# Retention's sample tokens in a hybrid decode step: keys copied to their placed columns ahead of the products, v summed and placed by one matrix

## The chip, the cores and the metric

One Trainium2 chip, one core. The metric is the device time of one execution in microseconds (us), the median of several runs. The core's engines run side by side, each through its own list of instructions in order: TensorE (PE for its matmuls, PEld for the loads of the stationary matrix), VectorE (DVE), ScalarE (ACT), GpSimd (POOL) and SyncE (SP), which here only issues transfers. Engines wait for each other through semaphores.

## The reference, cut to what matters

A two-layer decoder step with shared weights: a prompt of 512 tokens, and 32 sample tokens (8 sequences of 4 tokens each, at positions from 4096). Layer 1 mixes by retention, with 4 heads, keys of 256 and values of 512 elements; each sample sequence has a state `S` of 256 x 512 per head.

```python
def step(S, qkv):
    qc, kc, vc = qkv
    scores = jnp.einsum('bhid,bhjd->bhij', qc, kc) * decay
    inner = jnp.einsum('bhij,bhjv->bhiv', scores, vc)
    cross = jnp.einsum('bhid,bhdv->bhiv', qc, S) * cross_w[:, :, None]
    S_new = S * chunk_decay[:, None, None] + jnp.einsum('bhjd,bhjv->bhdv', kc * state_w[:, :, None], vc)
    return S_new, inner + cross
```

`q`, `k` (after a rotation by position) and `v` are projections of the normalized tokens. For a sample sequence there is one chunk of its 4 tokens. The outputs are all tokens after the decoder, the convolution states and the retention states, among them `S_new` of the eight sample sequences.

## The kernel before, in words

The kernel keeps tokens along the free side: 512 prompt columns and 32 sample columns, 544 in all. Each projection is made in three products of a high and a low part: a tensor is split into a rounded high part (`split`: ScalarE copies to the reduced type, L202) and the rest (VectorE subtracts, L203), and high x high, high x low and low x high are summed in PSUM. A scheduler orders the instructions of each engine from the program; `tc.issue_after` adds an order by hand.

The retention layer runs over the four heads, `h` from 0 to 3. In a head:

- `value` (its products stand on L1251 to L1253) multiplies the tokens by four pieces of the v weights, 24 products of 512 columns each, into four banks of PSUM. After each second piece it multiplies the sample tokens `xs` by the unsplit pieces (L1259), four products side by side in four strips of 32 output rows, so that the sum over the depth lies in four partial sums, one to a strip, in `pvs`. After the second piece it splits q and k, and calls `sample_scores` and `keys`. At the end `pvs` is scaled and split into `v4` (L1283, L1284), the four strips are added by the product with `sum4` (L1288), and the sum, 32 rows, is split into `v2`. Then the prompt's v is split into `vh`, `vl` (L1294, L1295).
- `sample_scores` multiplies the 32 sample keys by the 32 sample queries (L1434), masks and scales the result (`ss`, L1438 and L1439), splits it, and places it by two products with `places` (L1151, L1152, in `placed`) into 128 rows; ScalarE copies it to `scp` (L1443).
- `keys` transposes the prompt's keys (L1306) and splits them into `knh`, `knl`, and transposes the sample keys (L1315) and splits them into `k2`.
- `sample_operands` places `v2` and `k2` by four products with `places` (L1151, L1152), copies the first to `vs` (L1350) and multiplies the second by two row masks into `kns` (L1353).
- `state` makes the prompt's state (L175 to L177), `scores` its masked scores, `inner` its outputs.
- `sample_outputs` multiplies `vs` by `scp` (L1459) and the states by the queries `qm` (L1463); `states_update` adds `kns` times `vs` (L1481) to the scaled states (L1486, VectorE) and stores them.
- In heads 1 and 2 (`AHEAD`) the head before is projected in between (`held_parts`, which splits the gated outputs into `oldh`, `oldl`; `held_project`, L187), and each head but the last makes the next head's q (`qk_project`, L187).

The 128 placed rows are four groups of 32, for two sequences each, in places of 8 rows: for group g the rows hold the 8 tokens of the group three times over, and 8 rows of zeros. With v's places (high, low, high) and k's places (high, high, low) one product over a group's rows sums high x high, high x low and low x high. `places` holds four such placing matrices of 32 x 128 (two for v, two for k), loaded as a part of the constants `cb` into `where_p`.

```python
here = (n[:, None] // 8 == j[None] // 32) & (n[:, None] % 8 == j[None] % 8)
place = (j[None] % 32) // 8
for w, at in enumerate(((0, 2), (1,), (0, 1), (2,))):
    cb[:NS, 800 + w * P : 800 + (w + 1) * P] = here & np.isin(place, at)
```

PSUM has four single banks (`bank`, named sm) and two double ones (`psum`, named mm). `pvs` holds one double tile through all of `value`; the scores' tile, the prompt's transposed keys and the sample's transposed keys follow each other in the other. `where_p` and `mask_p` lie in a stretch of `cb` that the jobs ahead of this layer use as a weight buffer, so their loads (L1175, in `qk_loaded`) wait until that buffer is free.

Of the kernel before, what the change touches and what calls it, by code (L numbers as in the profile page):

```python
# [52 lines left out]
def hybrid_decode_kernel(ctx: ExitStack, tc: tile.TileContext, a: dict, o: dict):  # L53
# [1062 lines left out]
    with ExitStack() as c2:  # L1116
# [18 lines left out]
        part4 = one.tile([P, 2, NS], F32, tag="part4", name="part4")  # L1135
        for i in range(2):
            nc.vector.tensor_add(
                part4[:, i, :], ident[:, 2 * i * NS : (2 * i + 1) * NS], ident[:, (2 * i + 1) * NS : (2 * i + 2) * NS]
            )
        nc.vector.tensor_add(sum4, part4[:, 0, :], part4[:, 1, :])  # L1140
# [7 lines left out]

        def placed(out, hi, lo, w):

            nc.tensor.matmul(out, places[:, 2 * w, :], hi, start=True, stop=False)  # L1151
            nc.tensor.matmul(out, places[:, 2 * w + 1, :], lo, start=False, stop=True)  # L1152
# [15 lines left out]
        def qk_loaded(st):  # L1168
# [5 lines left out]
            for t, c in columns[:3]:  # L1174
                nc.sync.dma_start(t, a["cb"][:, c])  # L1175

            with tc.issue_after(last_mixed[0].ins):
# [6 lines left out]
                nc.vector.tensor_copy(places, where_p[:NS].rearrange("p (w c) -> p w c", w=4))  # L1184
# [54 lines left out]
        def value(h, st):  # L1239
# [47 lines left out]
            for i in range(2):  # L1287
                nc.tensor.matmul(pvs[:NS, 1, :], sum4, v4[:, i, :], start=(i == 0), stop=(i == 1))  # L1288
            v2 = [pool.tile([NS, DV], F32R, tag=f"rt{i}", name=nm("v2"), bufs=1) for i, pool in enumerate((kp, tp))]
            v2_split[0] = split(*v2, pvs[:NS, 1, :])  # L1290
# [8 lines left out]
            st["v"] = (vh, vl, v2)  # L1299

        def keys(h, st):
# [12 lines left out]
            for dt in range(2):  # L1314
                nc.tensor.transpose(pt[:NS, 0, token_tiles(dt)], krot[:, dt, SEQ:], ident)  # L1315
            k2 = qp.tile([NS, 2, 2 * P], F32R, tag="vs", name=nm("k2"), bufs=1)
            split(k2[:, 0, :], k2[:, 1, :], pt[:NS, 0, : 2 * P])
            st["kn"] = (knh, knl, k2)

        def state(h, st, c):  # L1320

            knh, knl, k2 = st["kn"]
            vh, vl, v2 = st["v"]
# [19 lines left out]

        def sample_operands(h, st):
            k2, v2 = st["kn"][2], st["v"][2]
            pt = psum()
            placed(pt[:, 0, :], *v2, 0)
            placed(pt[:, 1, : 2 * P], k2[:, 0, :], k2[:, 1, :], 1)
            vs = qp.tile([P, DV], F32R, tag="vs", name=nm("vs"), bufs=1)
            nc.scalar.activation(vs, pt[:, 0, :], AF.Copy)  # L1350
            kns = tp.tile([P, 2, 2 * P], F32R, tag="kns", name=nm("kns"), bufs=1)
            for r in range(2):
                nc.vector.tensor_scalar_mul(kns[:, r, :], pt[:, 1, : 2 * P], mask_r[:, r : r + 1])  # L1353
            st["vs"], st["kns"] = vs, kns
# [36 lines left out]
        def inner(h, st, it):  # L1391

            vh, vl, _ = st["v"]
# [35 lines left out]
        def sample_scores(h, st):  # L1429
# [3 lines left out]
            for dt in range(2):  # L1433
                nc.tensor.matmul(  # L1434
                    pt[:NS, 0, :NS], krot[:, dt, SEQ:], qrot[:, dt, SEQ:], start=(dt == 0), stop=(dt == 1)
                )
            ss = tp.tile([NS, NS], F32, tag="ss", name=nm("ss"), bufs=1)
            nc.vector.tensor_mul(ss, pt[:NS, 0, :NS], mask_s[:NS])  # L1438
            nc.vector.tensor_mul(ss, ss, st["gs"][:NS])  # L1439
# [105 lines left out]
        for h in range(NH):  # L1545
# [205 lines left out]
```

## Time and profile before

| | |
|---|---|
| runs | 1411.15, 1411.09 and 1410.4 us; median 1411.09 |
| profiled execution, first to last instruction | 1409.1 us |
| median of the runs less that span | 2.0 us |
| TensorE busy, matmuls | 1396.3 us, 99% |
| VectorE busy | 1132.7 us, 80% |
| ScalarE busy | 821.7 us, 58% |
| GpSimd busy | 213.9 us, 15% |
| granted TensorE clock, mean | 0.999 |

The profile is of one execution, which carries no time of its own beside its span. A row of the timeline has the start in us from the span's start, the time of the row in us, the engine, the line of the kernel, the operation, the tile written and the tiles read, for a matmul the shape of the array that it uses (rows*columns), the partitions x elements written, the type, and the number of instructions put together in the row. In brackets stands how long the engine was idle before it and what ended that. A float32 product whose operands aren't of the reduced type stands as two matmuls for each one of the program (L1259, L1434, L1463); a transpose is one. The retention heads lie from about 690 to 1010 us.

### The profile page before, as it was taken

Reading aid. Unit: us, or ns where it says so; the run is one execution under the profiler, and the core shown is the slowest. Engines: PE = TensorE matmul, PEld = TensorE weight load, DVE = VectorE, ACT = ScalarE, POOL = GpSimd, SP = SyncE. Lnnn points to the kernel's source line nnn. Section 1 sums busy time; section 2 is a strip of 40 time slices with the busy share of each in tenths; the row PEclk is TensorE's granted clock in tenths of the full one; section 3 lists DMA queues with packets and bytes.
Section 4 is the critical chain, followed back from the end, with each engine's and each line's share of the span. In section 5 each row is a group of like instructions: output and inputs, shape, how many; then the busy total and the mean of one; then the engine's idle time right before and its main releaser. Section 6 shows DMA issues by size and latency. Waiting matters only on the chain.

```text
span 1409.1 us, 26606 instructions
## 1 busy us (share of the span) xinstructions
PE 1396.3 (99%) x10476; PEld 1319.9 (94%) x10476; DVE 1132.7 (80%) x1929; ACT 821.7 (58%) x1281; POOL 213.9 (15%) x248
## 2 busy tenths in 40 slices
PE   9999999999999999999999999999999999999997
PEld 9999999999999999999877877887899999999997
DVE  6987879898989878767867586585798898989884
ACT  7666567677677557677532313213387767667654
POOL 0111011222221204111000000000111222121212
PEclk9999999999999999999999999999999999999999
DMA  6476347768686745677666365465676777777742
GB/s 206 121 166 166 107 110 158 173 163 185 143 196 149 171 108 158 176 199 203 197 216 232 120 212 179 139 240 179 201 152 151 168 170 172 154 184 157 163 108 87
DMA packets 99246, 233.82 MB, mean 166 GB/s; under 512 B 9744, under 2 KB 33312, under 8 KB 98736
## 3 DMA queue, kind: packets, MB, share of 16 engines
q1 hardware_dynamic: 67984, 167.60, 38.3%
q0 software_dynamic: 28688, 56.61, 23.5%
q10 hardware_dynamic: 2448, 7.91, 1.5%
q8 instruction: 82, 1.34, 0.4%
q14 instruction: 44, 0.36, 0.1%
HBM read 191.97 MB, written 28.42 MB: 156 GB/s over the span
## 4 chain that ended last, share of the span: by engine, by line
PE 93%; DVE 4%; DMA 1%; ACT 1%; issue 1%; POOL 0%; SPq 0%; DVEq 0%; POOLq 0%; ACTq 0%
PE sm L386 43%; PE mm L386 16%; PE mm L187 14%; PE sm L187 4%; PE sm L1251 2%; PE sm L1252 2%; PE sm L1253 2%; PE sm L175 2%; PE sm L177 2%; PE sm L176 1%; PE sm L1463 1%; DVE S L1486 1%; PE mm L1259 1%; PE mm L1412 0%; DVE ol L203 0%
## 5 line engine op out<-in xcount | busy, mean ns | idle before, releaser
L386 PE MATMUL sm<-oh,wh 128*128 128x272 f32 x856 | 247.8, 290 | 0.5 <-DVE b L447 0.5
L386 PE MATMUL sm<-ol,wh 128*128 128x272 f32 x856 | 246.2, 288 | 0.0
L386 PE MATMUL sm<-oh,wl 128*128 128x272 f32 x856 | 246.1, 287 | 0.0
L202 ACT ACTIVATE h<-w 128x1024 fp32r<-128x1024 f32 (+3 forms) x170 | 136.6, 804 | 105.8 <-PE mm L386 92.7
L203 DVE TENSOR_TENSOR l<-w,h 128x1024 fp32r<-128x1024 f32 (+3 forms) x170 | 153.5, 904 | 28.0 <-ACT h L202 25.0
L315 ACT ACTIVATE wh<-w 128x1024 fp32r<-128x1024 f32 (+1 forms) x134 | 133.7, 998 | 56.0 <-PE sm L386 48.3
L386 PEld LDWEIGHTS sm<-oh,wh 128*128 128x128 f32 x856 | 161.3, 188 | 2.0 <-DVE b L447 0.9
L386 PEld LDWEIGHTS sm<-oh,wl 128*128 128x128 f32 x856 | 161.1, 188 | 0.0
L386 PEld LDWEIGHTS sm<-ol,wh 128*128 128x128 f32 x856 | 160.9, 188 | 0.1
L386 PE MATMUL sm<-parts,wh 128*128 128x272 f32 x736 | 142.5, 288 | 0.0
L202 ACT ACTIVATE wh<-w 128x1024 fp32r<-128x1024 f32 (+3 forms) x76 | 67.6, 897 | 117.2 <-PE mm L187 62.0
L318 POOL DMA_DIRECT2D wl<-in_ffgu_dram x87 | 81.9, 941 | 327.9 <-ACT wl L317 135.5
L386 PE MATMUL mm<-oh,h 128*128 128x272 f32 x396 | 115.5, 292 | 0.0
L386 PEld LDWEIGHTS sm<-parts,wh 128*128 128x128 f32 x736 | 115.5, 188 | 0.0
L386 PE MATMUL mm<-oh,l 128*128 128x272 f32 x396 | 113.4, 286 | 0.0
L386 PE MATMUL mm<-ol,h 128*128 128x272 f32 x396 | 113.2, 286 | 0.0
L316 DVE TENSOR_TENSOR wl<-w,wh 128x512 fp32r<-128x512 f32 (+1 forms) x134 | 87.1, 650 | 26.5 <-ACT wh L315 26.2
L386 PE MATMUL sm<-parts,wl 128*128 128x272 f32 x368 | 106.1, 288 | 0.2 <-DMA wl<-in_rtqk_dram 0.2
L317 ACT ACTIVATE wl<-wh 128x512 fp32r<-128x512 f32 (+1 forms) x173 | 102.9, 595 | 2.0
L203 DVE TENSOR_TENSOR wl<-w,wh 128x1024 fp32r<-128x1024 f32 (+3 forms) x76 | 79.5, 1055 | 13.4 <-ACT wh L202 13.0
L187 PE MATMUL mm<-parts,wh 128*128 128x272 f32 x488 | 82.6, 291 | 0.9 <-ACT wh L202 0.9
L386 PE MATMUL sm<-oh,h 128*128 128x272 f32 x284 | 82.3, 290 | 0.3 <-ACT oh L202 0.2
(382 smaller groups left out, 3841.2 us busy)
## 6 DMA issues: line engine op xcount, KB each, us to landing
w<-in_ffgu_dram SPq DMA_DIRECT2D x66, 512.0 KB
wl<-in_ffgu_dram POOLq DMA_DIRECT2D x87, 256.0 KB, 5.2
S<-in_rets_dram SPq DMA_DIRECT2D x16, 1024.0 KB
out_rets_dram<-S SPq DMA_DIRECT2D x16, 1024.0 KB
w<-in_ffdn_dram SPq DMA_DIRECT2D x36, 384.0 KB
cb<-in_ffgu_dram SPq DMA_DIRECT2D x22, 512.0 KB
w<-in_cvin_dram SPq DMA_DIRECT2D x21, 512.0 KB
wl<-in_ffdn_dram POOLq DMA_DIRECT2D x48, 192.0 KB, 4.7
```

The lines of the kernel that those rows point to most:

```text
L175: nc.tensor.matmul(out, lh, rh, start=start, stop=False, skip_group_check=True)
L177: last_product[0] = nc.tensor.matmul(out, ll, rh, start=False, stop=stop, skip_group_check=True)
L187: last_product[0] = nc.tensor.matmul(half(pt, hf)[:, :HT], w[:, c], act[k][:, hf * HT : (hf + 1) * HT], start=(first and k == ks[0] and i ...
L202: h = nc.scalar.activation(dh, src, AF.Copy)
L203: last_low[0] = nc.vector.tensor_sub(dl, src, dh.bitcast(F32))
L315: nc.scalar.activation(wh, w, AF.Copy)
L316: last_mixed[0] = nc.vector.tensor_sub(wl[:, :n], w[:, :n], wh[:, :n].bitcast(F32))
L317: nc.scalar.activation(wl[:, n:], wh[:, n:].bitcast(F32), AF.Copy, scale=-1.0)
L318: nc.gpsimd.dma_start(wl[:, n:], src[:, 1, :] if len(src.shape) == 3 else src[:, n:], accum_op=ALU.add)
L386: last = nc.tensor.matmul(out, w[:, c], b, start=(first and j == 0 and i == 0), stop=(j == len(self.ks) - 1 and i == 2), skip_group_check= ...
L1251: nc.tensor.matmul(out, xh[kt][:, ts_], wh[:, cw], start=(kt == 0), stop=False)
L1252: nc.tensor.matmul(out, xh[kt][:, ts_], wl[:, cw], start=False, stop=False)
```

## The change

The score of the sample tokens is now made in 128 rows at once: ScalarE copies the rotated sample keys three times over to their placed columns in `kpl` (128 x 2 x 4 x 4 x 8, zeros in each fourth place), and the products with the queries (new L1452) give the placed scores. The transposes of the sample keys (new L1330) read `kpl` too and give placed keys. `v4` is multiplied by one 128x128 matrix `put` in place of `sum4`: it adds the four strips and puts the sum in all three places. High and low parts are then made from the placed results by row scales: ScalarE rounds the result times `sign` (1, -1 or 0 by row; for low rows the negative high part), and VectorE adds the result times a row mask for the low rows. `mask_put`, the score mask in placed rows, is made once, in head 0, by a product with `put`. `sample_operands`, `placed`, `places`, `k2` and `v2` go. `where_p` is loaded in four pieces of 32 partitions, the two v placing matrices for each strip, in place of all four for 32 rows; `put` is their sum.

```diff
-        places = one.tile([NS, 4, P], F32R, tag="places", name="places")
-
-        sum4 = one.tile([P, NS], F32R, tag="sum4", name="sum4")
...
-        nc.vector.tensor_add(sum4, part4[:, 0, :], part4[:, 1, :])
+        put = one.tile([P, P], F32R, tag="put", name="put")
+        kpl = one.tile([P, 2, 4, 4, 8], F32, tag="kpl", name="kpl")
+        nc.gpsimd.memset(kpl, 0.0)
+        mask_put = one.tile([P, NS], F32, tag="mput", name="mput")
+        place = one.tile([P, 4], F32, tag="place", name="place")
+        nc.vector.tensor_reduce(
+            place, ident.rearrange("p (g q c) -> p q g c", g=4, q=4), axis=mybir.AxisListType.XY, op=ALU.add
+        )
...
+        def signs():
+
+            both = one.tile([P, 1], F32, tag="both", name="both")
+            nc.gpsimd.tensor_tensor(both, place[:, 0:1], place[:, 2:3], op=ALU.add)
+            nc.gpsimd.tensor_tensor(sign[:, 0:1], both, place[:, 1:2], op=ALU.subtract)
+            nc.gpsimd.tensor_tensor(both, place[:, 0:1], place[:, 1:2], op=ALU.add)
+            nc.gpsimd.tensor_tensor(sign[:, 1:2], both, place[:, 2:3], op=ALU.subtract)
+            nc.gpsimd.tensor_tensor(sign[:, 2:4], mask_r, sign[:, 1:2].to_broadcast([P, 2]), op=ALU.mult)
+            nc.gpsimd.tensor_tensor(low_k, mask_r, place[:, 2:3].to_broadcast([P, 2]), op=ALU.mult)
...
-            for t, c in columns[:3]:
+            for t, c in (columns[0], columns[2]):
                 nc.sync.dma_start(t, a["cb"][:, c])
+            for g in range(4):
+                nc.sync.dma_start(where_p[g * NS : (g + 1) * NS, : 2 * P], a["cb"][:NS, 800 : 800 + 2 * P])
+            signs()
...
-                nc.vector.tensor_copy(places, where_p[:NS].rearrange("p (w c) -> p w c", w=4))
+                nc.vector.tensor_add(put, where_p[:, :P], where_p[:, P : 2 * P])
...
             for i in range(2):
-                nc.tensor.matmul(pvs[:NS, 1, :], sum4, v4[:, i, :], start=(i == 0), stop=(i == 1))
-            v2 = [pool.tile([NS, DV], F32R, tag=f"rt{i}", name=nm("v2"), bufs=1) for i, pool in enumerate((kp, tp))]
-            v2_split[0] = split(*v2, pvs[:NS, 1, :])
+                nc.tensor.matmul(pvs[:, 1, :], put, v4[:, i, :], start=(i == 0), stop=(i == 1))
+            vt = kp.tile([P, DV], F32R, tag="rt0", name=nm("vt"), bufs=1)
+            vs = st["vs"] = qp.tile([P, DV], F32R, tag="vs", name=nm("vs"), bufs=1)
+            v2_split[0] = nc.scalar.activation(vt, pvs[:, 1, :], AF.Copy, scale=sign[:, 0:1])
+            nc.vector.scalar_tensor_tensor(
+                vs, pvs[:, 1, :], place[:, 1:2], vt.bitcast(F32), op0=ALU.mult, op1=ALU.add
+            )
...
             for dt in range(2):
-                nc.tensor.transpose(pt[:NS, 0, token_tiles(dt)], krot[:, dt, SEQ:], ident)
-            k2 = qp.tile([NS, 2, 2 * P], F32R, tag="vs", name=nm("k2"), bufs=1)
-            split(k2[:, 0, :], k2[:, 1, :], pt[:NS, 0, : 2 * P])
+                nc.tensor.transpose(pt[:, 0, token_tiles(dt)], kpl[:, dt].rearrange("p g q c -> p (g q c)"), ident)
+            kns = st["kns"] = tp.tile([P, 2, 2 * P], F32R, tag="kns", name=nm("kns"), bufs=1)
+            kt = tp.tile([P, 2, 2 * P], F32R, tag="rt1", name=nm("kt"), bufs=1)
+            for r in range(2):
+                nc.scalar.activation(kt[:, r, :], pt[:, 0, : 2 * P], AF.Copy, scale=sign[:, 2 + r : 3 + r])
+            for r in range(2):
+                nc.vector.scalar_tensor_tensor(
+                    kns[:, r, :], pt[:, 0, : 2 * P], low_k[:, r : r + 1], kt[:, r, :].bitcast(F32),
+                    op0=ALU.mult, op1=ALU.add,
+                )
...
-        def sample_operands(h, st):
...
-            placed(pt[:, 0, :], *v2, 0)
-            placed(pt[:, 1, : 2 * P], k2[:, 0, :], k2[:, 1, :], 1)
...
             for dt in range(2):
+                nc.scalar.activation(
+                    kpl[:, dt, :, :3, :],
+                    krot[:, dt, SEQ:].rearrange("p (g c) -> p g c", g=4).unsqueeze(2).to_broadcast([P, 4, 3, 8]), AF.Copy,
+                )
+            if h == 0:
+                nc.tensor.matmul(pt[:, 1, :NS], put[:NS].bitcast(F32), mask_s[:NS], start=True, stop=True)
+                nc.scalar.activation(mask_put, pt[:, 1, :NS], AF.Copy)
+            for dt in range(2):
                 nc.tensor.matmul(
-                    pt[:NS, 0, :NS], krot[:, dt, SEQ:], qrot[:, dt, SEQ:], start=(dt == 0), stop=(dt == 1)
+                    pt[:, 0, :NS], kpl[:, dt].rearrange("p g q c -> p (g q c)"), qrot[:, dt, SEQ:],
+                    start=(dt == 0), stop=(dt == 1),
                 )
-            ss = tp.tile([NS, NS], F32, tag="ss", name=nm("ss"), bufs=1)
-            nc.vector.tensor_mul(ss, pt[:NS, 0, :NS], mask_s[:NS])
-            nc.vector.tensor_mul(ss, ss, st["gs"][:NS])
-            s2 = tp.tile([NS, 2, NS], F32R, tag="s2", name=nm("s2"), bufs=1)
-            split(s2[:, 0, :], s2[:, 1, :], ss)
-            placed(pt[:, 1, :NS], s2[:, 0, :], s2[:, 1, :], 1)
-            nc.scalar.activation(grouped(scp)[:, :, 0:8], grouped(pt[:, 1, :NS]), AF.Copy)
+            ss = tp.tile([P, NS], F32, tag="ss", name=nm("ss"), bufs=1)
+            nc.vector.tensor_mul(ss, pt[:, 0, :NS], mask_put)
+            nc.vector.tensor_mul(ss, ss, st["gs"])
+            s2 = tp.tile([P, NS], F32R, tag="s2", name=nm("s2"), bufs=1)
+            nc.scalar.activation(s2, ss, AF.Copy, scale=sign[:, 1:2])
+            nc.vector.scalar_tensor_tensor(
+                grouped(scp)[:, :, 0:8], grouped(ss), place[:, 2:3], grouped(s2.bitcast(F32)), op0=ALU.mult, op1=ALU.add
+            )
...
             fill(0)
-            sample_operands(h, st)
             state(h, st, 0)
```

In the order that the scheduler makes of the changed kernel, the score products take the place of the old ones in heads 1 to 3, right behind L1259; the eight transposes of the prompt's keys follow two value products behind them in every head. In head 0 the product of `mask_put` stands behind L1259 and two value products ahead of the scores. In heads 1 and 2 VectorE makes the second half of `oldl` ahead of the low half of the fourth v piece, where it stood behind it and behind one further weight split.

More of the change, by code (lines that the diff above doesn't have):

```diff
@@ L1314, in keys @@
             for dt in range(2):
[L1315 to L1318 removed]
+                nc.tensor.transpose(pt[:, 0, token_tiles(dt)], kpl[:, dt].rearrange("p g q c -> p (g q c)"), ident)
[8 more added lines that the diff above has]
+                )
+            st["kn"] = (knh, knl)
         def state(h, st, c):
[L1322 to L1323 removed]
+            knh, knl = st["kn"]
+            vh, vl = st["v"]
             if c == 0:
```

22 lines of the change are left out of this document (4 added, 18 removed).

## The prediction

> **What bounds the kernel now.** I read the page's busy times and chain first, then the busy times by stretch for the four heads of the retention layer (690 to 1010 us), where every edit lies.
>
> ```profile
> PE 1396.3 (99%) x10476; PEld 1319.9 (94%) x10476; DVE 1132.7 (80%) x1929; ACT 821.7 (58%) x1281; POOL 213.9 (15%) x248
> ...
> PE 93%; DVE 4%; DMA 1%; ACT 1%; issue 1%; POOL 0%; SPq 0%; DVEq 0%; POOLq 0%; ACTq 0%
> ```
>
> ```profile
> 729.00:766.00 37.00, 36.84 (x231) 28.38 (x228) 34.61 (x60) 5.77 (x6) 3.17 (x5) 1.00 0.70 232
> ...
> sum 320.00, PE 319.29 PEld 249.62 DVE 222.50 ACT 89.29 POOL 12.60; mean PE 45.61 PEld 35.66 DVE 31.79 ACT 12.76 POOL 1.80
> ```
>
> The columns of a stretch are its length, then PE, PEld, DVE, ACT and POOL busy, granted clock, DMA share and GB/s. TensorE is idle for 0.71 us of these 320 us, at full clock; VectorE has 97 us to spare and ScalarE 231. So TensorE's stream of instructions sets the end, and an edit is worth what it takes out of that stream, unless it makes a new wait. Busy matmul rows overlap each other, so I price by the distance from one start to the next, in the timeline of TensorE. Here is head 0 around the scores of the sample tokens:
>
> ```profile
> 701.97 1.06 PE L1259 MATMUL mm<-w,xs 128*32 128x512 f32 x8
> 702.86 0.29 PE L1434 MATMUL mm<-rot,rot 128*32 128x32 f32 x4
> 703.07 0.50 PE L1251 MATMUL sm<-wh,parts 128*128 128x512 f32 x1
> 703.41 0.40 PE L1252 MATMUL sm<-wl,parts 128*128 128x512 f32 x1
> ...
> 703.88 0.40 PE L1251 MATMUL sm<-wh,parts 128*128 128x512 f32 x1
> 704.20 0.28 PE L1151 MATMUL mm<-s,places 32*128 32x32 f32 x1
> 704.41 0.50 PE L1252 MATMUL sm<-wl,parts 128*128 128x512 f32 x1
> 704.84 0.28 PE L1152 MATMUL mm<-s,places 32*128 32x32 f32 x1
> 705.05 0.50 PE L1253 MATMUL sm<-wh,parts 128*128 128x512 f32 x1
> 705.39 0.40 PE L1251 MATMUL sm<-wh,parts 128*128 128x512 f32 x1
> 705.62 1.04 PE L1306 MATMUL mm<-cb,rot 128*128 128x128 f32 x8
> 706.41 0.48 PE L1252 MATMUL sm<-wl,parts 128*128 128x512 f32 x1
> 706.73 0.40 PE L1253 MATMUL sm<-wh,parts 128*128 128x512 f32 x1
> ...
> 709.05 0.38 PE L1315 MATMUL mm<-cb,rot 128*32 128x128 f32 x2
> 709.19 0.48 PE L1251 MATMUL sm<-wh,parts 128*128 128x512 f32 x1
> 709.51 0.39 PE L1252 MATMUL sm<-wl,parts 128*128 128x512 f32 x1
> ```
>
> A product of 512 columns in the full 128*128 shape follows the last at 0.23 us (0.47 for two from 703.41 to 703.88, of which one is left out; 705.39 to 705.62). A small product in a 32*128 shape costs far more than its 32 columns: the array loses time going into the other shape and coming back.
>
> **What is removed.** *Score placing*, two products per head: from 703.88 to 705.39 pass 1.51 us, in which three regular products take 0.69. The two cost 0.82 us, and in four heads 3.28.
>
> *v and k placing*, four products per head, in head 0 and then in head 2:
>
> ```profile
> 720.35 0.62 PE L1288 MATMUL mm<-v,sum 128*32 128x512 f32 x2
> 720.81 0.28 PE L176 MATMUL sm<-qkhl,qkhl 128*128 128x256 f32 x1
> ...
> 721.40 0.28 PE L175 MATMUL sm<-qkhl,qkhl 128*128 128x256 f32 x1
> 721.65 0.49 PE L1151 MATMUL mm<-v,places 32*128 32x512 f32 x1
> 722.07 0.50 PE L175 MATMUL sm<-vh,knh 128*128 128x512 f32 x1
> ...
> 723.61 0.50 PE L175 MATMUL sm<-vh,knh 128*128 128x512 f32 x1
> 723.95 0.39 PE L176 MATMUL sm<-vl,knh 128*128 128x512 f32 x1
> 724.17 0.40 PE L177 MATMUL sm<-vh,knl 128*128 128x512 f32 x1
> ```
>
> ```profile
> 880.94 0.41 PE L187 MATMUL mm<-oldl,wh 128*128 128x272 f32 x2
> 881.18 0.41 PE L187 MATMUL mm<-oldh,wl 128*128 128x272 f32 x2
> ...
> 882.41 0.50 PE L176 MATMUL sm<-vl,knh 128*128 128x512 f32 x1
> 882.75 0.39 PE L177 MATMUL sm<-vh,knl 128*128 128x512 f32 x1
> ```
>
> In head 0 the 256-column product at 721.40 (0.12, half of 0.23) ends its slot at 721.52; up to 724.17 pass 2.65 us, and five regular 512-column products stand in it (1.15), so the four cost 1.50. In head 2 they stand together: from 881.42 (881.18 and 0.24 for such a pair) to 882.75 pass 1.33, less one regular 0.23: 1.10. Head 3 is issued like head 0 (split in two places), head 1 like head 2: 2 x 1.50 + 2 x 1.10 = 5.20. Removed in all: 8.48 us.
>
> **What is added on TensorE.** *Scores* (new name: kpl times the rotated q): still two products in two passes each, but the stationary side is now 128 columns wide, in the full shape. The nearest row is a product with 128x128 weights and one moving column:
>
> ```profile
> 1052.14 0.50 PE L272 MATMUL mm<-cb,sqacc 128*128 128x1 f32 x4
> 1052.50 0.37 PE L386 MATMUL sm<-oh,h 128*128 128x272 f32 x1
> ```
>
> Four such passes take 0.36. Now L1259 and the scores take 701.97 to 703.41 less one regular product: 1.21. After: L1259's 0.89, leaving its 128*32 shape 0.11 (0.34 instead of 0.23 at 703.07), four passes 0.36, and 0.09 for the first product behind short ones (0.32 at 706.41): 1.45. That is +0.24 per head, 0.96 in all. Bounds: nothing dearer than today's narrow passes (0), or 0.21 for each pass, as from 704.84 to 705.05: 0.48 more per head, 2.9 in all. I take 0.96, since the row has the same weights.
>
> The Trainium skill, TensorE: Matmul & The Clock Gate, section "LDWEIGHTS (loading the stationary operand)", speaks against this edit: a weight load lasts by its columns, not its rows, about columns / 1.2 ns, so 107 ns for 128 against 27 for 32. By that an estimate for the sixteen passes is 1.3 us more, and the sum would end 0.3 us higher; the rows show 0.09 us a pass against 0.05, and I stay with them.
>
> *Key transposes* (L1315): today 0.46 less 0.23 = 0.23 per head; after, two full-shape transposes at 0.10 (0.79 for eight at 705.62) and 0.09 behind: 0.29. +0.24 in all; bounds 0 and 1.2 (0.21 each and 0.11 behind). *The sum of v* with put for sum4 (L1288): two products of 512 columns, 0.46 = 2 x 0.23 now and after; bounds 0 and 0.11 per head, 0.45. *mask_put*, once, in head 0: a 32-row product in two passes, with two value products between it and the scores. One placing product is 0.41 (half of 0.82); a second pass and another short series bring it to 0.5; bounds 0.2 and 0.8.
>
> The Trainium skill, TensorEngine Tiling (Array Packing), section "Key Properties", says that a change of tiling mode drains TensorE. The placing rows agree, 0.41 us for 32 columns; L1288, 128*32 between full-shape products, doesn't (0.46 us for two); by the rule alone the new v sum would save some tenths more.
>
> **Off the path.** ScalarE gets two kpl copies, two kt and one vt, and loses s2's low chain, the scp copy, k2 and vs; VectorE loses the k and v low parts and two kns multiplies and gets two kns and one vs of the new kind. Both have the idle time of the sum row, and no waiting TensorE instruction stands directly behind them except in two places. First, the scores' PSUM tile is freed by the multiply ss, and the eight key transposes, two regular products behind the scores (0.23 each) in heads 1 to 3, need that tile. Second, in heads 1 and 2 VectorE now does oldl's second half before the low half of the last v weights:
>
> ```profile
> 769.09 0.18 DVE L1438 TENSOR_TENSOR ss<-mm,cb 32x32 f32<-32x32 f32 x1 [4.06 <-PE mm L1434]
> ...
> 771.52 1.04 PE L1306 MATMUL mm<-cb,rot 128*128 128x128 f32 x8
> ...
> 773.71 1.22 DVE L203 TENSOR_TENSOR knl<-mm,knh 128x1024 fp32r<-128x1024 f32 x1 [3.76 <-ACT knh L202]
> ...
> 777.46 1.27 DVE L203 TENSOR_TENSOR oldl<-gate,oldh 128x1088 fp32r<-128x1088 f32 x1
> ```
>
> In the first, ss took 0.18 after 4.06 us of idle VectorE; the transposes follow the scores after 0.09 + 0.46, so ss fits. In the second, knl starts 2.19 us after the transposes, so knl, oldl and a 1.2 us split end 5.9 us after them; TensorE needs that half after 22 regular products (5.1) and ten transposes (1.1), 6.2 later. It fits by 0.3 us; I take no wait, bounds 0 and 0.5 per head, 2.0. At the start SyncE issues four quarter loads of the constants in place of one, with the next v weights' load queued behind them, and VectorE's put waits for all four; all of it stands before the last job's products are over, which cover it. POOL gets one memset and six tiny operations behind the two memsets, and the first score scaling on ScalarE waits for them:
>
> ```profile
> wl<-in_ffgu_dram POOLq DMA_DIRECT2D x87, 256.0 KB, 5.2
> ...
> 735.23 0.57 POOL L248 TENSOR_TENSOR rs<-rs,expo 128x1 f32<-128x1 f32 x1 [44.25 <-DVE mv L1385]
> ```
>
> POOL has stood idle for 44 us here, since 691; six operations at 0.57 are 3.4 us, and the scaling comes at about 704. Without their covers the loads would cost one landing (5.2 us, the page's median for 256 KB on another queue), and POOL's steps 3.4, each once. On the gain side TensorE's 0.71 us of idle could go too.
>
> **Sum.** -8.48 + 0.96 + 0.24 + 0.5 = -6.78 us. The profiled span 1409.1 becomes 1402.3; the median of the runs, 1411.09, lies 2.0 above that span, so I forecast 1404.3. All low ends: -8.48 + 0.2 - 0.71 = -9.0, 1402.1. All high ends: -8.48 + 2.9 + 1.2 + 0.45 + 0.8 + 2.0 = -1.1, 1410.0; that all of them meet is unlikely.
>
> **The rivals.** *Short full-shape passes are dear*: 0.21 for each score pass and transpose, 0.8 for mask_put: -8.48 + 2.9 + 1.2 + 0.8 = -3.6, 1407.5. For it: a short product's weights can't hide behind a long stream. Against it: the four passes in 0.36.
>
> *The freed time is lost to another pace*: loads of states and weights set the heads' pace, and TensorE waits where it worked: 1411. For it: DMA at 0.70 from 729 to 766, VectorE busy for 34.61 of 37 us there. Against it: TensorE would show waits already, and shows 0.71 us in four heads.
>
> *Slower: the transposes stand still behind VectorE.* The PSUM tile of the scores went free through ScalarE after four value products; now the transposes come two products behind the scores. VectorE leaves the full stretch just ahead of ss with a row of long passes (low halves of q, of the weights, of oldl: 1.2 us each, and some gating, some 4.4 us as an estimate). If it does these only when the scores are done, each of heads 1 to 3 loses 4.4 us: -6.8 + 13.2, 1417.5. It begins to cost when VectorE is over 4.06 us later than now, and turns the sign 2.3 us after that. Against it: VectorE waits for TensorE in each head, so a lead can't pile up.
>
> **How the numbers follow.** Forecast 0.80 (own range 1402.1 to 1407.1, the upper end with the waits, mask_put and the v sum at their bounds), dear passes 0.08, other pace 0.07, slower 0.05. The range 1402.2 to 1407.9 holds both of the first two. Two runs of this kernel can be told apart at 0.2%, 2.8 us: faster means under 1408.3. The first two cases give 0.88, of which 0.02 go to "same" for waits that add up: faster 0.86, same 0.09, slower 0.05.
>
> **What would show it.** Right: no 32*128 rows but mask_put and L1481's; the scores at about 1.45 from L1259's start to the next regular product's slot; the heads shorter by 1.5, 1.6, 1.6 and 2.0 us in their order; TensorE idle still under 2 us in the heads. Wrong: idle ahead of the eight transposes with ss as releaser (the slower case), ahead of the last v products with wl as releaser (the 0.3 us slack), or waits for S or w loads that grow by what the placing products gave up (other pace).

## The result, and the profile after

| | before | changed |
|---|---|---|
| median of 5 runs, us | 1411.09 (1409.88 to 1411.31) | 1404.51 (1404.06 to 1405.36) |
| span of the profiled execution, us | 1409.1 | 1403.6 |
| ratio of the runs, 95% interval | | 0.9958 (0.9946 to 0.9969) |

The changed kernel is faster by 0.4%, more than the 0.2% that two runs can tell apart. The page's busy times and its chain of waits show that no other engine took over:

```profile
PE 1390.2 (99%) x10454; PEld 1317.3 (94%) x10454; DVE 1132.1 (81%) x1923; ACT 822.9 (59%) x1286; POOL 219.4 (16%) x255
...
PE 93%; DVE 2%; issue 2%; DMA 2%; POOL 0%; ACT 0%; SPq 0%; DVEq 0%; POOLq 0%; ACTq 0%
```

TensorE's busy time fell by 6.1 us, VectorE's and ScalarE's hardly moved, and 93% of the chain is TensorE's, as before. Where in the layer the time went shows in the busy times by stretch, cut at the first value product of each head and, for the last head, at the last gated transposes. First the kernel before, then the changed one (columns: length, busy time of PE, PEld, DVE, ACT and POOL with the instructions of each, granted clock, DMA share, GB/s):

```profile
690.76:756.11 65.35, 65.19 (x375) 48.42 (x374) 50.66 (x89) 20.84 (x30) 2.86 (x6) 1.00 0.68 232
756.11:846.76 90.65, 90.52 (x573) 73.16 (x571) 60.97 (x96) 23.80 (x32) 2.71 (x5) 1.00 0.51 176
846.76:937.29 90.53, 90.36 (x572) 73.03 (x570) 60.75 (x96) 23.62 (x32) 2.72 (x5) 1.00 0.53 182
937.29:1008.30 71.01, 70.75 (x408) 52.55 (x407) 48.90 (x88) 20.48 (x30) 4.17 (x7) 1.00 0.55 191
```

```profile
691.08:754.89 63.81, 63.68 (x371) 48.05 (x370) 49.92 (x85) 21.57 (x34) 8.77 (x13) 1.00 0.70 237
754.89:844.16 89.27, 89.11 (x566) 72.39 (x565) 60.80 (x95) 24.03 (x33) 2.70 (x5) 1.00 0.52 178
844.16:933.80 89.64, 89.22 (x567) 72.40 (x565) 60.80 (x95) 24.05 (x33) 2.71 (x5) 1.00 0.53 184
933.80:1002.79 68.99, 68.73 (x402) 51.92 (x400) 48.93 (x87) 20.68 (x29) 4.18 (x7) 1.00 0.58 196
```

The heads are shorter by 1.54, 1.38, 0.89 and 2.02 us, 5.83 in all; 1.52, 1.62, 1.62 and 2.02 had been forecast. Heads 0 and 3 are as worked out, head 1 lacks 0.24 and head 2 lacks 0.73. In head 2 TensorE is idle for 0.42 us (89.64 less 89.22), where it was 0.17. Two questions are left for the experiments: what head 2 lost, and whether the prices behind the terms that came out are the right ones.

The timeline of TensorE in the changed kernel, head 0, from the strip products of the sample tokens (L1270, L1259 before) to the product behind the scores:

```profile
702.30 1.07 PE L1270 MATMUL mm<-w,xs 128*32 128x512 f32 x8
703.29 0.41 PE L1449 MATMUL mm<-cb,put 32*128 32x32 f32 x2
703.63 0.50 PE L1262 MATMUL sm<-wh,parts 128*128 128x512 f32 x1
703.97 0.39 PE L1263 MATMUL sm<-wl,parts 128*128 128x512 f32 x1
704.20 0.53 PE L1452 MATMUL mm<-rot,kpl 128*128 128x32 f32 x4
704.56 0.47 PE L1264 MATMUL sm<-wh,parts 128*128 128x512 f32 x1
704.88 0.40 PE L1262 MATMUL sm<-wh,parts 128*128 128x512 f32 x1
```

and in head 1, which has no mask product:

```profile
766.66 1.07 PE L1270 MATMUL mm<-w,xs 128*32 128x512 f32 x8
767.65 0.63 PE L1452 MATMUL mm<-rot,kpl 128*128 128x32 f32 x4
768.12 0.47 PE L1262 MATMUL sm<-wh,parts 128*128 128x512 f32 x1
768.43 0.40 PE L1263 MATMUL sm<-wl,parts 128*128 128x512 f32 x1
```

The row shape is left only in the mask's product, once, and in the state updates. The four score passes take 0.36 us in head 0 (704.20 to 704.56), as forecast, but 0.47 in head 1 (767.65 to 768.12), and the same in heads 2 and 3. From L1270's start in head 1 to the end of the product behind the scores pass 1.77 us; less a regular 0.23 that is 1.54, where 1.45 was forecast and 1.21 stood before.

Most of head 2's idle time stands in front of gated transposes (timeline of TensorE, changed kernel):

```profile
922.08 0.66 PE L1422 MATMUL mm<-cb,yn 128*128 128x128 f32 x4 [0.26 <-DVE gate L1428]
```

VectorE, which must multiply the gate first, came late from the rotation of the next head's keys (L1226), which waited for their load (timeline of VectorE, changed kernel):

```profile
916.69 0.73 DVE L1226 TENSOR_TENSOR rt<-rot,sqlast 128x544 f32<-128x544 f32 x1 [0.95 <-DMA rot<-km]
```

On SyncE's queue that load stands behind the load of a state, and this one waits 0.8 us until a store of the states has landed. First the changed kernel, then the kernel before (columns: start, time of issue):

```profile
902.68 0.39 SPq L1508 DMA_DIRECT2D out_rets_dram<-S  x1
906.47 0.33 SPq L1613 DMA_DIRECT2D gate<-gm  x1
907.66 0.38 SPq L1471 DMA_DIRECT2D S<-in_rets_dram  x1
908.13 0.46 SPq L1604 DMA_DIRECT2D rot<-km  x1
```

```profile
910.82 0.43 SPq L1451 DMA_DIRECT2D S<-in_rets_dram  x1
911.95 0.32 SPq L1585 DMA_DIRECT2D rot<-km  x1
```

Before the change neither load waited for a store, and VectorE took up the rotation at 919.61 without a wait for it. The keys' load is now issued 3.82 us earlier, and VectorE wants it at 915.74 (916.69 less 0.95), 3.87 earlier. That difference makes only 0.05 of the 0.95 us. The rest is a later landing: 8.56 us behind the issue, where it was at most 7.66. The state's load ahead of it moved by only 3.16 us, because of the store, so the keys' load now follows it at 0.47 us in place of 1.13. Whether that order makes it late is what run 8 asks.

### The profile page after: what moved, and what is told of

Same layout as the page of the kernel before. It is cut to its first block, busy times and chain, and to the rows that moved or that the text cites. A ratio compares the mean times of both kernels' runs of the same rounds, so it can differ in the third digit from the quotient of the medians.

```text
span 1403.6 us, 26578 instructions
## 1 busy us (share of the span) xinstructions
PE 1390.2 (99%) x10454; PEld 1317.3 (94%) x10454; DVE 1132.1 (81%) x1923; ACT 822.9 (59%) x1286; POOL 219.4 (16%) x255
## 4 chain that ended last, share of the span: by engine, by line
PE 93%; DVE 2%; issue 2%; DMA 2%; POOL 0%; ACT 0%; SPq 0%; DVEq 0%; POOLq 0%; ACTq 0%
PE sm L386 43%; PE mm L386 16%; PE mm L187 14%; PE sm L187 4%; PE sm L1262 2%; PE sm L1264 2%; PE sm L1263 2%; PE sm L175 2%; PE sm L177 1%; PE sm L176 1%; PE sm L1483 1%; DVE S L1506 1%; PE mm L1270 1%; DMA wl<-in_rtout_dram 1%; PE mm L1422 0%
```

## The experiments

The lengths of the heads in all runs, measured as above, in us:

| run | head 0 | head 1 | head 2 | head 3 | sum | median of the runs | wait for the keys' load, head 2 |
|---|---|---|---|---|---|---|---|
| before | 65.35 | 90.65 | 90.53 | 71.01 | 317.54 | 1411.09 | none |
| changed | 63.81 | 89.27 | 89.64 | 68.99 | 311.71 | 1404.51 | 0.95 |
| 1, changed again | 64.43 | 89.26 | 89.52 | 69.06 | 312.27 | 1405.50 | 0.84 |
| 2, v and k alone | 64.02 | 89.78 | 90.38 | 69.61 | 313.79 | 1407.18 | 1.14 |
| 3, slow scaling | 63.81 | 89.57 | 90.27 | 69.04 | 312.69 | 1405.45 | 1.33 |
| 4, keys' load on ScalarE | 64.33 | 93.69 | 89.54 | 69.04 | 316.60 | 1411.00 | 1.52 (head 1: 4.36) |
| 5, row products added | 66.93 | 92.29 | 92.31 | 72.12 | 323.65 | 1417.67 | 0.39 |
| 6, full products added | 64.66 | 90.01 | 90.01 | 69.85 | 314.53 | 1407.80 | none |
| 7, strip products added | 64.66 | 90.06 | 90.00 | 69.87 | 314.59 | 1408.30 | none |
| 8, keys' load first | 63.84 | 89.27 | 89.25 | 69.03 | 311.39 | 1404.68 | none |
| 9, scores later | 64.04 | 89.28 | 89.29 | 69.02 | 311.63 | 1405.11 | none |

Beside these the kernel before had medians between 1410.70 and 1410.89.

### 1. The changed kernel again

No edit.

> The changed kernel once more, to tell what recurs. Theory A (the lost part of head 2's gain is built into the order of the loads): head 2, from its first value product to head 3's, is again 0.7 to 1.1 us shorter than before instead of 1.62, with VectorE's rotation of the next keys (L1226) again waiting some 0.5 to 1.0 us for the keys' load; the time is within 1.0 us of 1404.5. Theory B (an accident of that one execution): the wait is gone, head 2 is 1.3 to 1.6 us shorter, and the span is about 0.5 us below 1403.6.

Head 2 came out 1.01 us shorter than before, with a wait of 0.84: theory A, it recurs. The median is 1405.50, ratio 0.9963 (0.9951 to 0.9975). Head 0 was 0.62 longer than in the first execution. There ScalarE waited 1.76 us for a load of v weights where it had waited 1.04, VectorE was 0.7 us later from then on, and TensorE idled 0.29 and 0.17 us ahead of gated transposes. So, between these two executions, a few tenths of a microsecond in a head come and go with the landing of loads, by way of VectorE, which is near full behind the middle of head 0.

### 2. The new way for v and k alone

```diff
-                    pt[:, 0, :NS], kpl[:, dt].rearrange("p g q c -> p (g q c)"), qrot[:, dt, SEQ:],
-                    start=(dt == 0), stop=(dt == 1),
+                    pt[:NS, 0, :NS], krot[:, dt, SEQ:], qrot[:, dt, SEQ:], start=(dt == 0), stop=(dt == 1)
...
-            nc.scalar.activation(s2, ss, AF.Copy, scale=sign[:, 1:2])
...
+            split(s2[:, 0, :], s2[:, 1, :], ss)
+            for i in range(2):
+                nc.tensor.matmul(pt[:, 1, :NS], places[:, i, :], s2[:, i, :], start=(i == 0), stop=(i == 1))
+            nc.scalar.activation(grouped(scp)[:, :, 0:8], grouped(pt[:, 1, :NS]), AF.Copy)
```

> The new way for v and k, with the scores left in their old form (32 rows, two placing products). Theory (the terms of the prediction add up): the heads lose 1.50, 1.10, 1.10 and 1.50 us of placing and gain 0.06 of transposes each, so 4.96 below before: 1406.1; against the changed kernel it is 1.5 to 1.8 us longer, since each head keeps 0.82 of score placing and is spared 0.24 to 0.35 for scores on 128 columns, and the one product for the mask. Rival 1 (the freed time is mostly taken by loads that are due at a fixed pace): less than 3 us below before. Rival 2 (the scores' part is lost again in dearer passes): equal to the changed kernel within 0.5 us.

It is 3.6 us below before (ratio 0.9972, 0.9962 to 0.9982), not 4.96, and 1.7 above run 1, as the terms said. Its heads are shorter than before by 1.33, 0.87, 0.15 and 1.40, where the terms gave 1.44, 1.04, 1.04 and 1.44. So three heads come within 0.2 of the forecast, and head 2 alone lacks 0.89, with VectorE's wait for the keys' load at 1.14. The rival that loads take the freed time holds in this one place and not as a pace for all heads.

### 3. VectorE holds the scores' PSUM tile longer

```diff
-            nc.vector.tensor_mul(ss, pt[:, 0, :NS], mask_put)
+            for _ in range(7):
+                nc.vector.tensor_mul(ss, pt[:, 0, :NS], mask_put)
```

> The changed kernel with VectorE's first scaling of the scores (L1457) done seven times over, six multiplications of 128x32 more, some 1.2 us in each head before the next use of the scores' PSUM tile is free. It asks what stands behind the slower rival, that TensorE's eight transposes of the keys wait for VectorE's reading of the scores. In the changed kernel one such wait of 0.2 us is shown in all. Theory A (the slack there is under 0.5 us): the wait ahead of the transposes (L1321's place) grows by 0.7 to 1.2 us in each head, and the time by 3 to 5 us. Theory B (the slack is over 1.5 us and VectorE's later work hides the rest): no wait grows, the time is within 0.5 us of the changed kernel.

The time is that of run 1 within 0.1 us, so theory B by the number, but not by its reason. The timeline of TensorE in head 1 of this run, from the scores to the transposes:

```profile
767.30 0.63 PE L1452 MATMUL mm<-rot,kpl 128*128 128x32 f32 x4
...
769.68 0.39 PE L1264 MATMUL sm<-wh,parts 128*128 128x512 f32 x1
769.91 1.03 PE L1321 MATMUL mm<-cb,rot 128*128 128x128 f32 x8
```

The transposes now come nine products behind the scores, and in the changed kernel two: the scheduler gave a different order to the kernel with the longer scaling. TensorE shows no wait at the transposes, since value products stand ahead of them. Some of VectorE's extra 1.3 us a head shows elsewhere: head 2 is 0.63 us longer than in the changed kernel, with the wait for the keys' load at 1.33 and TensorE idle for 0.63 ahead of the gated transposes, where it was 0.26. What the scaling would cost with the order held fixed was not tried.

### 4. The keys' load on ScalarE's queue

```diff
-                nc.sync.dma_start(nxt["rot"][1], k_made[h + 1])
+                nc.scalar.dma_start(nxt["rot"][1], k_made[h + 1])
```

> The changed kernel with the load of the next head's rotated keys issued on ScalarE's queue instead of SyncE's, where it stands behind a states' load that waits for a store to land. Theory A (the place in SyncE's queue makes it late): VectorE's wait of 0.95 us for it in head 2 is gone, head 2 is some 0.45 us shorter, and the time 0 to 0.5 us below the changed kernel. Theory B (the transfer itself is slow, as the DMA engines are at 0.77 of their time there): the wait stays within 0.3 us of what it was, and so does head 2. Theory C (ScalarE reaches the issue later than SyncE does): the wait grows, and the time with it, by up to 1 us a head.

Theory C by its sign, for the wait grows, but dearer than thought and not by its reason, a later issue: 1411.00 (1408.64 to 1416.01), ratio 1.0005 (0.9996 to 1.0014), the whole gain gone. In head 1 SyncE issued the 1 MB of a state at 817.45 and the 1 MB of the gate at 818.14, and ScalarE the 544 KB of the keys at 818.35. The timelines of VectorE and, in the second fence, of TensorE:

```profile
828.35 0.73 DVE L1226 TENSOR_TENSOR rt<-rot,sqlast 128x544 f32<-128x544 f32 x1 [4.36 <-DMA rot<-km]
```

```profile
835.14 1.12 PE L1422 MATMUL mm<-cb,yn 128*128 128x128 f32 x4 [2.97 <-DVE gate L1428]
836.19 1.90 PE L1483 MATMUL sm<-S,qm 128*8 128x512 f32 x8
838.02 0.52 PE L177 MATMUL sm<-mid,qkhl 128*128 128x512 f32 x1
```

The keys' load, the smallest of the three, took 10.0 us from its issue to its use. In the changed kernel it was issued at 818.78, at the same place in the head (63.89 us from its start, here 63.86), but on SyncE's queue and ahead of the gate's load, and it was there when VectorE took it up at 826.36. VectorE's order had changed too: here the rotation stood one normalization earlier, so that more of VectorE's work was behind the wait. How much is the transfer and how much the order was not told apart. The head is 4.42 us longer. TensorE's idle time makes 2.97 of it. The twelve instructions behind it (L1422 and L1483) make most of the rest: they took 2.88 us from 835.14 to 838.02, at a granted clock of 0.50 in that stretch, where they took 1.55 at full clock in the changed kernel (832.45 to 834.00). In head 2 ScalarE issued the keys' load 0.43 us ahead of the state's, at 912.03, and it was still used only 7.17 us later, after a wait of 1.52. A queue of its own was no way past the other loads.

### 5 to 7. The price of short products in three shapes

Each of these adds 32 products whose result nobody reads, eight per head; they differ in the operands and the output only. Run 5, with rows:

```diff
+                        if c == 1:
+                            with tc.issue_after(last.ins):
+                                nc.tensor.matmul(pvs[:, 1, :NS], put[:NS], put[:NS, :NS], start=True, stop=True, skip_group_check=True)
```

The product in run 6, in the full shape, and in run 7, with 32 columns of weights:

```diff
+                                nc.tensor.matmul(pvs[:, 1, :NS], put, put[:, :NS], start=True, stop=True, skip_group_check=True)
```

```diff
+                                nc.tensor.matmul(pvs[:NS, 1, :NS], put[:, :NS], put[:, :NS], start=True, stop=True, skip_group_check=True)
```

> The changed kernel with 32 products added (8 a head, each behind the third product of a value tile of the second piece), of the removed placing's shape: weights and data on 32 rows, 128 columns of weights, 32 columns of data; nobody reads their result. Theory A (what the change took away was the entry to and the exit from the 32-row shape, not the columns): 0.4 us each, as the mask's product in head 0 has (0.34 from its start to the next one's), so 11 to 13 us more than the changed kernel. Theory B (any short product costs about its weights' load): 0.1 to 0.2 each, 3 to 6 us in all, and the same as the full-shape ones.

> The same 32 products in the full shape (weights 128 x 128, 32 columns of data), between full-shape products. Theory A: only their own passes, 0.12 us each (the score's passes in head 0 took 0.36 for four, 0.09 each), so 3 to 4 us more than the changed kernel, a quarter to a third of the row-shaped ones. Theory B: the same as the row-shaped ones within 1 us.

> The same 32 products with 32 columns of weights on all 128 rows, 32 columns of data: the shape of the old score product and of the strip products just ahead of it. Theory A (a change of column shape costs as a change of row shape does): 0.35 to 0.45 us each, 11 to 14 us more than the changed kernel, which would also explain why the score passes behind a strip product took 0.47 instead of 0.36. Theory B (a narrower output alone costs nothing): at most as the full-shape ones, 2 to 4 us.

The timeline of TensorE in head 0, with rows, then full, then strip:

```profile
697.16 0.40 PE L1264 MATMUL sm<-wh,parts 128*128 128x512 f32 x1
697.49 0.28 PE L1267 MATMUL mm<-put 32*128 32x32 f32 x1
697.69 0.50 PE L1262 MATMUL sm<-wh,parts 128*128 128x512 f32 x1
698.03 0.40 PE L1263 MATMUL sm<-wl,parts 128*128 128x512 f32 x1
```

```profile
697.70 0.39 PE L1264 MATMUL sm<-wh,parts 128*128 128x512 f32 x1
697.93 0.18 PE L1267 MATMUL mm<-put 128*128 128x32 f32 x1
697.96 0.48 PE L1262 MATMUL sm<-wh,parts 128*128 128x512 f32 x1
698.28 0.39 PE L1263 MATMUL sm<-wl,parts 128*128 128x512 f32 x1
```

```profile
696.93 0.40 PE L1264 MATMUL sm<-wh,parts 128*128 128x512 f32 x1
697.17 0.18 PE L1267 MATMUL mm<-put 128*32 128x32 f32 x1
697.19 0.48 PE L1262 MATMUL sm<-wh,parts 128*128 128x512 f32 x1
697.51 0.40 PE L1263 MATMUL sm<-wl,parts 128*128 128x512 f32 x1
```

Read from L1264's start to L1263's: 0.87 with the row product, 0.58 with the full one, 0.58 with the strip; two regular products alone take 0.46. So a row-shaped product costs 0.41, the other two 0.12 each. Theory A of run 5 holds. The 0.41 are 0.10 ahead of it (0.33 to its start where 0.23 is regular), 0.20 in its own slot and 0.11 behind (0.34 for the next). Theory A of run 7 falls: 32 columns of weights on all 128 rows cost no more than the full shape, so the change of column shape alone doesn't explain the 0.47 of the score passes. The 32 row products lengthen the four heads by 11.94 us (forecast 11 to 13), the full ones by 2.82 and the strips by 2.88; by the medians of the runs it is 13.2, 3.3 and 3.8 us.

The heads show something more: runs 6 and 7 add 0.85, 0.74 and 0.86 (0.85, 0.79 and 0.88) to heads 0, 1 and 3, but 0.37 (0.36) to head 2, and there VectorE's wait for the keys' load is gone. What is added to head 2 fills the wait. That is the second sign that this load lengthens head 2 by some tenths. In run 5 VectorE still waits 0.39 us for it, but TensorE shows no wait for the gate.

### 8. The keys' load ahead of the state's

```diff
-            states_load(h, st, 3)
             fill(3)
...
                 nc.sync.dma_start(nxt["rot"][1], k_made[h + 1])
+            states_load(h, st, 3)
```

> The changed kernel with the load of the last of a head's four states issued behind the load of the next head's rotated keys instead of ahead of it; on SyncE's queue that changes places in head 2 alone. The run on ScalarE's queue put the keys' load behind the gate's and VectorE waited 4.36 us for it in head 1, so the bytes queued ahead of it decide, not the engine that issues it. Theory A (the states' 1 MB ahead of it makes the keys' load late in head 2): VectorE's wait there (0.95, 0.84, 1.14 and 1.33 us in four runs) is gone, head 2 goes from 89.64 and 89.52 to some 88.9 to 89.2 us, and the time 0.3 to 0.7 us below the changed kernel, under what the runs can tell. Theory B (the transfer has the DMA engines full whatever the order): the wait is the same within 0.3 us. Theory C (the states' load is late in its place): a new wait of TensorE for it ahead of the last sample outputs of head 2, and no gain.

The queue of SyncE in head 2, and VectorE's rotation:

```profile
907.10 0.32 SPq L1603 DMA_DIRECT2D rot<-km  x1
907.52 0.39 SPq L1471 DMA_DIRECT2D S<-in_rets_dram  x1
```

```profile
912.67 0.72 DVE L1226 TENSOR_TENSOR rt<-rot,sqlast 128x544 f32<-128x544 f32 x1
```

Theory A: the keys are there at the latest 5.57 us after their issue, VectorE waits no more, the idle time ahead of the gated transposes is gone, and head 2 is 89.25, 0.27 to 0.39 below the two executions of the changed kernel and just above the 88.9 to 89.2 forecast. No wait for the state's load came in its place, so theory C falls. The keys' load was issued only 0.11 us earlier in the head (63.86 us from its start, where it was 63.97), so it is the place ahead of the state's load that brought the keys in time. VectorE's order changed as well: the rotation now stands ahead of a normalization, at 912.67, and even there the keys were ready. The profiled span is 1402.7, the shortest of the profiled ones, but the five executions of the changed kernel span 1402.3 to 1403.6; the median, 1404.68 (ratio 0.9955, 0.9942 to 0.9969), can't be told from the changed kernel's, as foreseen. By its profile it is the best of these versions, by its time no better than the changed kernel.

### 9. The scores behind a value product

To the kernel of run 8:

```diff
-                    sample_scores(h, st)
...
-                    keys(h, st)
-                    if h in AHEAD:
-                        held_parts(h, older)
...
+            def samples():
+                sample_scores(h, st)
...
+                        if kt == 4 and tt == 0:
+                            with tc.issue_after(last.ins):
+                                samples()
```

The new function holds the same calls; it stands behind the first value tile of the third piece.

> The kernel of the run before (keys' load first), with the scores, and what follows them in the code, moved from right behind the strip products to behind the first value tile of the third piece. It asks why four score passes took 0.47 us in heads 1 to 3 and 0.36 in head 0. Theory A (the weights of the first pass are loaded under the product ahead of it where that has 512 columns, and cannot be under strip products): in all four heads the score passes take 0.35 to 0.37, the strip products 0.88 to 0.90 to the next product's start where it was 0.99, and heads 1 to 3 are 0.1 to 0.2 us shorter each; the time stays within what the runs can tell, 0.2 to 0.6 below. Theory B (four such passes just cost 0.47 there, head 0 was an accident of its place): 0.47 in heads 1 to 3 again.

The timeline of TensorE in head 1:

```profile
766.01 1.06 PE L1286 MATMUL mm<-w,xs 128*32 128x512 f32 x8
767.01 0.50 PE L1275 MATMUL sm<-wh,parts 128*128 128x512 f32 x1
767.34 0.39 PE L1276 MATMUL sm<-wl,parts 128*128 128x512 f32 x1
767.57 0.40 PE L1277 MATMUL sm<-wh,parts 128*128 128x512 f32 x1
767.81 0.53 PE L1457 MATMUL mm<-rot,kpl 128*128 128x32 f32 x4
768.17 0.47 PE L1275 MATMUL sm<-wh,parts 128*128 128x512 f32 x1
768.49 0.40 PE L1276 MATMUL sm<-wl,parts 128*128 128x512 f32 x1
```

Half of theory A holds, and the other half falls. The score passes take 0.36 to 0.37 in all four heads. But the strips still take 1.00 to the next start, and the value product behind them now pays 0.33 (767.01 to 767.34) where the score passes had paid. From L1286's start to 768.49 pass 2.48; less the three value products that stand here in addition (0.69), 1.79 against 1.77. Nothing is gained: heads 1 to 3 have the lengths of run 8, and head 0 is 0.2 longer. So behind the eight strip products 0.11 is lost twice, up to the next start (1.00, where it is 0.88 to a product of their own shape: 701.95 to 702.83 in run 2) and once more in whatever comes next. What loses it is open: the two products of L1288 in the kernel before, in one strip, show neither part (0.46 for both, and the regular 0.12 for the product of 256 columns behind them).

## Why the prediction was right, point by point

- *TensorE's stream sets the end, and an edit is worth what it takes from it.* Right. TensorE's busy time fell by 6.1 us, the span by 5.5, and eight added row products lengthen heads 0, 1 and 3 by 3.0 to 3.1 us, where eight times 0.41 would be 3.3 (run 5).
- *v and k placing, 5.20 us, less the key transposes.* Right to 0.2 in three heads: 1.33 of 1.44, 0.87 of 1.04 and 1.40 of 1.44 (run 2). In heads 1 and 2 the same products before and after the placing stood 1.08 and 1.09 us closer together in the changed kernel, where 1.10 was the price. There 0.13 went the other way, where the first products of 272 columns follow those of 512 behind the v sum (0.65 from 875.12 to 875.77 in head 2, and 0.52 from 878.15 to 878.67 before); why is open.
- *Score placing, 0.82 per head.* The price behind it, 0.41 for a row-shaped product, is shown by run 5.
- *The sum of v, nothing.* Right: its two products take 0.46 to 0.47 in the changed kernel, 0.46 before.
- *Scores, +0.24 per head.* Too small: +0.33 in heads 1 to 3 (1.54 against 1.21). The step charged 0.11 for leaving the strips' shape and 0.36 for four passes, the row of four passes behind a product of the full shape. The passes took 0.47 because a second part of 0.11 is lost behind the strips, which run 9 moved onto another product without saving it. In all that is 0.3 to 0.4 us. What the Trainium skill says in TensorE: Matmul & The Clock Gate, section "LDWEIGHTS (loading the stationary operand)", charges a weight load by its columns; by the estimate made from it the sum would have ended 0.3 us higher, which is nearer. But the same passes take 0.36 away from the strips (run 9), so the difference came of their place. For passes in a row the traces agree in kind (0.21 for the four passes of 32 columns at 702.86 before, 0.36 to 0.47 for four of 128); where a product stands alone between long ones they do not, with 0.12 for 32 columns (run 7) and for 128 (run 6).
- *mask_put, +0.5.* It took 0.34 from its start to the next one's, once: 703.29 to 703.63. From the strips to the product behind the scores head 0 takes 0.35 more than head 1, with the two more value products taken off. Head 0, with this term too large and the scores' too small, came out at 1.54.
- *Key transposes, +0.06 per head.* 0.03 in head 0, where L1330 and the product behind it take 0.49 in the changed kernel (708.57 to 709.06) and 0.46 before, and 0.05 to 0.06 in the others.
- *No new waits.* Right for the two places that were named: VectorE's scaling and the low half of the last v weights hold up nothing, and TensorE's products show no wait on either. The scaling fits just in time: the weight load of the key transposes waits for it, 0.17 us in head 1 and 0.8 in the four heads, under the products ahead. Wrong for the one that was not: VectorE reaches the keys' rotation in head 2 before their load, which costs 0.3 to 0.4 us (0.27 to 0.39 come back in run 8). The step had listed the loads that set a pace as those of states and weights, as a rival for all heads; it was the load of the keys, queued behind a state's, in one head. Its bound of 0.5 per head for waits holds it.
- *The sum, -6.78 for a span of 1402.3.* The profiled spans were 1403.6 and 1404.9, but each of these two executions was the slowest of its five; the medians of the spans are 1402.7 and 1403.3. So the sum was 0.4 to 1.0 too large by the spans, and 0.2 to 1.5 by the shift of the medians of the time, 6.6 and 5.3 us. The runs show 0.3 to 0.4 of it in the scores, less 0.2 in mask_put, 0.3 in the order of products in heads 1 and 2 and 0.3 to 0.4 in the keys' load; the rest comes and goes with loads that land later in one execution than in another (run 1, head 0). The 2.0 us added for the distance of the median from the span set a median beside the span of another execution. Taken execution by execution the time lies 1.7 to 1.8 above the span in most runs, so that this term was some 0.2 too large, against a sum that took too much away. The two errors have opposite signs, so part of the agreement at 1404.5 is luck.
- *The rivals.* Dear short passes (0.21 each) fall: a full-shape pass is 0.12 (run 6). A pace set by loads is true in head 2 alone. The slower case, transposes standing behind VectorE, shows no idle time of TensorE: VectorE waits for the scores in each head, 4.08 to 4.49 us in heads 0 to 2, but only 0.37 in head 3, so it is ahead, there not by much. Run 3 could not put it to the test at a fixed order.

## What to carry to other kernels

Price a short matmul by its shape and its neighbours: here one on 32 rows between full-shape products cost 0.41 us, one on all 128 rows 0.12, with 32 columns of weights as with 128, so copying an operand onto all rows on an idle engine pays for itself where the products are many. Moving a short product away from a costly neighbour (the strips of run 9) did not remove the cost, which fell on the product that came in its place. When TensorE gets shorter by a microsecond, look at the loads that landed just in time before, with what is queued ahead of each; a transfer that is needed first should be issued ahead of the large ones, and a second queue gave it no precedence in the one run that tried it.

## What the runs showed of the hardware that was not expected

- Row shape and column shape are not alike. A product on 32 rows cost 0.41 us between full-shape ones, a product of 32 columns on 128 rows 0.12, as much as the full shape. The Trainium skill, TensorEngine Tiling (Array Packing), section "Key Properties", says that changing the tiling mode drains TensorE; the row product agrees with it, the single strip product and the two of L1288 in the kernel before do not show it, and the eight strip products of the sample tokens may, with 0.11 twice behind them.
- A load of 544 KB on ScalarE's queue, issued 0.21 us behind 1 MB on SyncE's, was used only 10.0 us after its issue, with a wait of 4.36 us (run 4, head 1). Issued 0.43 us ahead of the state's load, still on ScalarE's queue, it was used 7.17 us after its issue, with a wait of 1.52 (run 4, head 2); 0.42 us ahead of the state's load on SyncE's own queue it took at most 5.57 us (run 8, head 2).
- Behind the 2.97 us in which TensorE stood idle in run 4, the granted clock was 0.50 from 835.10 to 838.00 us, and the products there took 1.33 us more than at full clock. Behind the 0.63 us of idle time in run 3 (922.63) it stayed at 1.00.
- The first of POOL's small operations behind the memsets took 2.6 us in seven of the ten traces that have it, 6.45 in two and 0.19 in one. In the changed kernel all six took 5.8 us, where the prediction reckoned 3.4, and were done 7.9 us ahead of their first use (4.0 in run 1), so that it cost nothing here.
